# A convolution stage with a written VectorE order, norm terms with an operand in PSUM, and column sums one gate projection earlier

## The chip, the cores and the metric

The kernel runs on 1 core of one Trainium2 chip. The metric is the device time of one execution in microseconds. The core's engines work side by side and meet through semaphores: TensorE (PE in the profile, its weight loads PEld), VectorE (DVE), ScalarE (ACT), GpSimd (POOL) and SyncE (SP), which issues the transfers here.

## What is computed

Two layers over 256 tokens of width 2048: forgetting attention, then a causal convolution module. The change is in the second layer:

```python
def conv_mixer(h, w_in, b_in, dw, dw_b, ln_g, ln_b, w_out):
    proj = h @ w_in + b_in                       # h = rmsnorm(x) here; w_in is 2048 x 6144
    a, b, gate = jnp.split(proj, [C, 2 * C], axis=-1)        # C = 2048
    u = a * jax.nn.sigmoid(b)
    u = lax.conv_general_dilated(u, dw, ..., padding=[(30, 0)], feature_group_count=C) + dw_b   # 31 taps a channel
    u = jax.nn.silu(layernorm(u, ln_g, ln_b))    # mean and variance over the 2048 channels
    y = u * jax.nn.silu(gate)
    return y @ w_out
```

The result is added to the layer's input, and a final rmsnorm follows.

## The kernel before

The second layer holds channels on the partitions: a channel tile (`ct`, 16 of them) is 128 channels by 256 tokens. Each weight tile of 128 x 2048 numbers comes from memory into `raw`, ScalarE rounds it to `hi` (L93), VectorE or GpSimd makes the rest `lo` (L94), and TensorE does three matmuls for each product: hi by hi, hi by the activations' rest, lo by hi (L161). `hi` and `lo` have three buffers each. The order of TensorE is the order in which the program is written, for the whole kernel.

The stage runs in groups. Group 0 and group 1 are 128 channels wide, then come pairs 1 to 7 of 256 channels (two channel tiles). Each projects `b`, then `a`; VectorE evicts both (`eb`, `ea`, L669, times the token scales `rb1`), ScalarE makes the sigmoid of `b` in PSUM (L683), VectorE the gated input `u` (L684), into a PSUM bank with 30 zeros ahead (L682), and then 31 taps for each channel tile (L694, the first of group 0 and 1 L692). ScalarE writes the finished tile to `dall` (L699) and its square to `sq` (L705); GpSimd sums these over the tiles into `accd` and `accs`, VectorE the last ones (L712). To keep the squares small, the mean over the first 128 channels is taken with one matmul (`mean_shift`, `pm`, L722) and taken off everywhere (`negs`).

After the pairs come the four gate chunks of 512 channels (16 steps each, a step is a 128-deep slice of the weights), whose evicts `eg` go through a SiLU, and then the out projection (L188 to L190, `po`). The column sums `ln_rows` (`pstat`, L618) are put by an agenda (`at`) at step 9.5 of chunk 3; behind them come VectorE's small rows, GpSimd's power `rl` (L759), the row scales (VectorE's diagonals `dg`, TensorE's `bc_rl` and `bc_mr`, VectorE's copies to `rlb` and `mrb`) and the norm terms `t` with the results `y1a` and `y1b`.

TensorE has 4 banks of PSUM for projections and 4 for the rest. VectorE's order is a scheduler's: the evicts and the gated inputs stand under `tc.high_priority(2000)`, which puts them among the taps. GpSimd's order is the written one from chunk 3 on.

Of the kernel before, what the change touches and what calls it, by code (L numbers as in the profile page):

```python
# [19 lines left out]
MASK = 1.0e30  # L20
RMS_EPS = 1e-6
LN_EPS = 1e-5
LN_STEP = 9.5
LN_ROWS = 1.5


@with_exitstack
def tile_hybrid_trunk(
# [33 lines left out]
    def bank(name):  # L62
        return psa.tile([P, 512], F32, tag="at", name=name)
# [105 lines left out]
    def proj_t(wv, c0, width, ah, al, lo_engs, pieces=1, banks_apart=False, ahead=False, made=()):  # L169

        ps = banks_t(width)
        tail = []
        for kt, hv, lv in stream(wv, c0, width, lo_engs, pieces, ahead, made):
            if banks_apart and kt >= KT - 2048 // width:

                products_t(ps, kt, hv, lv, ah, al, range(2))
                tail.append((kt, hv, lv))
            else:
                products_t(ps, kt, hv, lv, ah, al, range(width // P))
        for kt, hv, lv in tail:  # L180
            products_t(ps, kt, hv, lv, ah, al, range(2, width // P))
        return ps
# [9 lines left out]
    def tiles(t):  # L192
        return lambda kt: t[:, kt, :]
# [468 lines left out]
    def evict(ps, width, name):  # L662

        outs = []
        for b, bank_ in enumerate(ps):
            n = min(2, width // P - 2 * b)
            e = ph.tile([P, 2, S], F32, tag="ev", name=f"{name}_{b}", bufs=4)
            with tc.high_priority(2000):
                nc.vector.tensor_tensor(  # L669
                    e[:, 0:n, :],  # L670
                    bank_[:, 0 : n * S].rearrange("p (a t) -> p a t", a=n),
                    rb1.broadcast_to([P, n, S]),
                    op=ALU.mult,
                )
# [3 lines left out]
    def conv_tile(ct, a, b, sig):

        u = bank(f"u{ct}")[:, 0 : TAPS - 1 + S]  # L680
        with tc.high_priority(2000):
            nc.vector.memset(u[:, 0 : TAPS - 1], 0.0)  # L682
            nc.scalar.activation(sig, b, AF.Sigmoid, bias=bT[:, KT + ct : KT + ct + 1])  # L683
            nc.vector.scalar_tensor_tensor(  # L684
                u[:, TAPS - 1 :], a, bT[:, ct : ct + 1], sig, op0=ALU.add, op1=ALU.mult
            )
        acc = ph.tile([P, S], F32, tag="acc", name=f"acc{ct}", bufs=3)
        for t in range(TAPS):
            w = dwT[:, t * KT + ct : t * KT + ct + 1]
            src = u[:, t : t + S]  # L690
            if t == 0 and ct < 2:
                nc.vector.tensor_scalar(acc, src, w, None, op0=ALU.mult)  # L692
            else:
                nc.vector.scalar_tensor_tensor(  # L694
                    acc, src, w, negs if t == 0 else acc, op0=ALU.mult, op1=ALU.add
                )
        bcol = dwbT[:, ct : ct + 1]
        d = dall[:, ct, :]
        nc.scalar.activation(d, acc, AF.Identity, bias=bcol)  # L699
        if ct < 2:  # L700
            shifted.append(d)
            return
        if ct % 2 == 0:
            sqs.append(ph.tile([P, 2, S], F32, tag="sq", name=f"sq{ct}", bufs=3))
        nc.scalar.activation(sqs[-1][:, ct % 2, :], acc, AF.Square, bias=bcol)  # L705
        if ct % 2 and ct < KT - 1:
            nc.gpsimd.tensor_tensor(accd, dall[:, 0:2, :] if ct == 3 else accd, dall[:, ct - 1 : ct + 1, :], op=ALU.add)
            nc.gpsimd.tensor_tensor(accs, accs, sqs[-1], op=ALU.add)
        if ct >= KT - 3:

            for acc, last in ((accd, d), (accs, sqs[-1][:, ct % 2, :])):
                nc.vector.tensor_tensor(  # L712
                    acc[:, 0, :], acc[:, 0, :], acc[:, 1, :] if ct == KT - 3 else last, op=ALU.add
                )

    shifted = []
    sqs = []

    def mean_shift():

        pm = bank("pm")[:, 0:S]
        nc.tensor.matmul(pm, ones, dall[:, 0, :], start=True, stop=True)  # L722
        nc.vector.tensor_scalar(negs, pm, -1.0 / P, None, op0=ALU.mult)
        for i, d in enumerate(shifted):
            nc.vector.tensor_tensor(d, d, negs, op=ALU.add)
            nc.scalar.activation(accs[:, i, :], d, AF.Square)

    def conv_group(c0, width):
        eng = VE if c0 < 256 else GE
        pc = 4 if c0 < 256 else 1  # L730
        pb = proj_t(w_cin, D + c0, width, tiles(ah), tiles(al), eng, pc)
        pa = None if c0 else proj_t(w_cin, c0, width, tiles(ah), tiles(al), eng, pc)
# [12 lines left out]
    rlb = ph.tile([P, 1, S], F32, name="rlb", bufs=1)  # L745
    mrb = ph.tile([P, 1, S], F32, name="mrb", bufs=1)

    def ln_rows():
        st = const.tile([P, 4], F32, name="st")
# [3 lines left out]
        nc.vector.tensor_scalar(st, pstat[:, 0:4], 1.0 / D, None, op0=ALU.mult)  # L753
        var = const.tile([P, 2], F32, name="var")
        nc.vector.tensor_tensor(var, st[:, 0:2], st[:, 0:2], op=ALU.mult)
        nc.vector.tensor_tensor(var, st[:, 2:4], var, op=ALU.subtract)
        nc.vector.tensor_scalar(var, var, 0.0, LN_EPS, op0=ALU.max, op1=ALU.add)
# [3 lines left out]
        nc.vector.tensor_tensor(mr, st[:, 0:2], rl, op=ALU.mult)
        at(LN_ROWS, lambda: row_scales(rl, rlb[:, 0, :], "rl"))
        at(LN_ROWS, lambda: row_scales(mr, mrb[:, 0, :], "mr"))
        at(LN_ROWS + 0, lambda: [gated(cp) for cp in range(4)])
# [38 lines left out]
    while agenda:
        agenda.pop(0)[1]()
# [130 lines left out]
```

## Time and profile before

| | us |
|---|---|
| median of 3 runs | 918.09 (917.91 to 918.62) |
| the profiled execution | 918.69 |
| its span, first to last instruction | 916.9 |
| TensorE busy in the span | 883.0 (96%) |
| VectorE / ScalarE / GpSimd busy | 597.8 / 414.7 / 373.1 |
| mean granted clock of TensorE | 0.983 of full speed |

The convolution stage runs from about 511 us to the end. The page's slices of the span show TensorE full up to some 780 us, then one slice of 40 at four tenths of its time, where its clock is at six tenths, and again full until the end. VectorE is at eight to nine tenths from 530 to 830 us.

### The profile page before, as it was taken

How to read it: one execution, taken by the hardware profiler on the slowest of the kernel's cores; microseconds unless marked ns; L12 is line 12 of the kernel's file. 1: busy time of each engine (PE TensorE's matmuls, PEld its weight loads, DVE VectorE, ACT ScalarE, POOL GpSimd, SP SyncE). 2: the span in 40 equal slices, each digit the busy share in tenths (PEclk: the TensorE clock that was granted, in tenths of full speed). 3: DMA queues.
4: the chain of work that ended last, by engine and by line, in shares of the span. 5: the costliest groups of instructions: out<-in, count | busy, mean ns of one | idle time of the engine just before them, and what ended most of it. 6: DMA issues, size and time to landing. Idle time of an engine off the chain costs nothing.

```text
span 916.9 us, 15886 instructions
## 1 busy us (share of the span) xinstructions
PE 883.0 (96%) x6642; PEld 849.8 (93%) x6642; DVE 597.8 (65%) x1042; ACT 414.7 (45%) x535; POOL 373.1 (41%) x234
## 2 busy tenths in 40 slices
PE   8799999999999999999999999999999999489996
PEld 8789899999999899989999999999999999477886
DVE  5464564445544564446655789988889879898541
ACT  5453554345534453346444534434433543266531
POOL 3128343103410232103100087989889888532110
PEclk9989999999999999999999999999999999689999
DMA  9899965689799756754455745555555555226532
GB/s 215 163 179 180 232 190 146 183 180 182 144 179 186 193 141 170 184 189 167 149 185 149 230 144 179 184 185 184 185 184 184 184 184 184 92 92 212 170 124 93
DMA packets 101563, 157.71 MB, mean 172 GB/s; under 512 B 4740, under 2 KB 42740, under 8 KB 101364
## 3 DMA queue, kind: packets, MB, share of 16 engines
q1 hardware_dynamic: 101156, 155.63, 63.1%
q8 instruction: 52, 0.85, 0.4%
q10 hardware_dynamic: 336, 1.07, 0.3%
q14 instruction: 19, 0.16, 0.1%
HBM read 154.59 MB, written 2.10 MB: 171 GB/s over the span
## 4 chain that ended last, share of the span: by engine, by line
PE 84%; DVE 5%; issue 3%; SPq 2%; DMA 2%; POOL 2%; ACT 1%; POOLq 0%; DVEq 0%; ACTq 0%
PE pt L161 63%; PE pv L189 3%; PE pv L188 3%; PE pv L190 3%; PE po L189 2%; PE po L190 2%; PE po L188 2%; SPq L313 2%; DMA rawk<-in_fox_w_in_dram 1%; DVE acc L694 1%; DMA raw<-in_fox_w_in_dram 1%; POOL lo L94 1%; ACT hi L93 1%; PE sc L485 1%; DVE t L777 1%
## 5 line engine op out<-in xcount | busy, mean ns | idle before, releaser
L161 PE MATMUL pt<-ah,hi 128*128 128x256 f32 x1472 | 422.0, 287 | 6.1 <-ACT hi L93 6.1
L93 ACT ACTIVATE hi<-raw 128x2048 fp32r<-128x2048 f32 (+2 forms) x188 | 271.4, 1465 | 343.5 <-PE pt L161 182.8
L161 PE MATMUL pt<-ah,lo 128*128 128x256 f32 x1472 | 419.0, 285 | 0.2 <-DVE lo L94 0.2
L161 PE MATMUL pt<-al,hi 128*128 128x256 f32 x1472 | 418.8, 284 | 0.0
L94 DVE TENSOR_TENSOR lo<-raw,hi 128x2048 fp32r<-128x2048 f32 (+1 forms) x136 | 216.1, 1611 | 201.7 <-ACT hi L93 201.7
L161 PEld LDWEIGHTS pt<-ah,hi 128*128 128x128 f32 x1472 | 285.1, 194 | 6.6 <-ACT hi L93 6.5
L161 PEld LDWEIGHTS pt<-ah,lo 128*128 128x128 f32 x1472 | 284.7, 193 | 0.6 <-DVE lo L94 0.6
L161 PEld LDWEIGHTS pt<-al,hi 128*128 128x128 f32 x1472 | 285.1, 194 | 0.0
L94 POOL TENSOR_TENSOR lo<-raw,hi 128x2048 fp32r<-128x2048 f32 (+1 forms) x52 | 223.8, 4316 | 61.0 <-ACT hi L93 60.6
L694 DVE SCALAR_TENSOR_TENSOR acc<-u,dwT,acc 128x256 f32<-128x256 f32 x480 | 196.8, 474 | 1.4
L161 PE MATMUL pt<-yh,hi 128*128 128x256 f32 x256 | 73.3, 286 | 0.0
L161 PE MATMUL pt<-yl,hi 128*128 128x256 f32 x256 | 72.5, 283 | 0.6 <-POOL yl L94 0.6
L161 PE MATMUL pt<-yh,lo 128*128 128x256 f32 x256 | 72.5, 283 | 0.0
L479 POOL CAST la<-ones 64x256 fp32r<-64x256 f32 x16 | 6.3, 394 | 143.0 <-PE sc L488 139.0
L188 PE MATMUL pv<-hi,ah 128*128 128x512 f32 x128 | 50.1, 391 | 0.0
L161 PEld LDWEIGHTS pt<-yl,hi 128*128 128x128 f32 x256 | 49.1, 192 | 0.8 <-POOL yl L94 0.8
L189 PE MATMUL pv<-hi,al 128*128 128x512 f32 x128 | 49.8, 389 | 0.0
L190 PE MATMUL pv<-lo,ah 128*128 128x512 f32 x128 | 49.8, 389 | 0.0
L161 PEld LDWEIGHTS pt<-yh,hi 128*128 128x128 f32 x256 | 49.1, 192 | 0.0
L161 PEld LDWEIGHTS pt<-yh,lo 128*128 128x128 f32 x256 | 49.1, 192 | 0.0
L200 POOL TENSOR_TENSOR r_l<-ms_l,mhalf 128x2 f32<-128x2 f32 x2 | 1.4, 714 | 99.5 <-DVE ms_l L198 99.5
L94 POOL TENSOR_TENSOR yl<-y,yh 128x256 fp32r<-128x256 f32 x15 | 19.8, 1322 | 42.1 <-ACT yh L93 42.1
(240 smaller groups left out, 1025.1 us busy)
## 6 DMA issues: line engine op xcount, KB each, us to landing
raw<-in_fox_w_in_dram SPq DMA_DIRECT2D x60, 1024.0 KB, 6.8
raw<-in_conv_w_in_dram SPq DMA_DIRECT2D x48, 1024.0 KB, 5.2
raw<-in_fox_w_out_dram SPq DMA_DIRECT2D x16, 1024.0 KB, 5.1
raw<-in_conv_w_out_dram SPq DMA_DIRECT2D x16, 1024.0 KB, 5.1
rawk<-in_fox_w_in_dram SPq DMA_DIRECT2D x4, 512.0 KB, 12.6
xn<-in_x_dram SPq DMA_DIRECT2D x3, 512.0 KB, 11.4
rawk<-in_fox_w_in_dram SPq DMA_DIRECT2D x4, 256.0 KB, 7.2
raw<-in_fox_w_in_dram SPq DMA_DIRECT2D x2, 512.0 KB, 15.4
```

The costliest lines, as they stand in the source:

```text
L93: nc.scalar.activation(dst_hi, src, AF.Copy)
L94: lo_eng.tensor_tensor(dst_lo, src, dst_hi.bitcast(F32), op=ALU.subtract)
L161: nc.tensor.matmul(ps[nt // 2][:, (nt % 2) * S : (nt % 2 + 1) * S], w[:, nt * P : (nt + 1) * P], a(kt), start=(kt == 0 and i == 0 and nt % ...
L188: nc.tensor.matmul(ps, ah(kt)[:, ms], hv, start=first, stop=False)
L189: nc.tensor.matmul(ps, al(kt)[:, ms], hv, start=False, stop=False)
L190: nc.tensor.matmul(ps, ah(kt)[:, ms], lv, start=False, stop=last)
L200: nc.gpsimd.tensor_tensor(r, ms, mhalf, op=ALU.pow)
L313: nc.sync.dma_start(bf[0:H], fox_b_f[0].rearrange("(h o) -> h o", o=1))
L479: nc.gpsimd.tensor_copy(la[0:64], ones[0:64, 0:1].broadcast_to([64, S]))
L485: nc.tensor.matmul(sc[:, 0:S], qT[q][:, j, :], kT[k][:, j, :], start=(i == 0), stop=False)
L694: nc.vector.scalar_tensor_tensor(acc, src, w, negs if t == 0 else acc, op0=ALU.mult, op1=ALU.add)
L777: nc.vector.tensor_tensor(t, dall[:, cs, :], rlb.broadcast_to([P, 2, S]), op=ALU.mult)
```

## The change

VectorE gets a written order from group 0's evicts to the end of gate chunk 0. The taps of a pair are collected in a list (`line`) and emitted with 8 entries held back (7 taps and the closing step); then come the next pair's evicts, then the 8, then the next pair's gated inputs. In front of chunk 0's evicts 30 entries are held back. `conv_alone` (channel tiles 0 and 1) uses two accumulators in turn and adds them at the end, one operand in PSUM. `mean_shift` is called at step 7 behind group 0, which is inside group 1's a-projection, and its result stays in a bank of its own (`kept`), so the others have 3 banks. `shift` reads it there. The last pair's sums go over a PSUM bank (`pd`, `ps`). The `lo` of group 1 are made by GpSimd. The column sums are at step 10 of chunk 2, the row scales four steps later; their diagonals are made by ScalarE, the results stay in PSUM, and `t` is there too.

```diff
-LN_STEP = 9.5
-LN_ROWS = 1.5
+LN_STEP = 10
+LN_ROWS = 4
...
-    psa = ctx.enter_context(tc.tile_pool(name="psa2", bufs=4, space=bass.MemoryType.PSUM, reuse_waits="tile"))
+    psa = ctx.enter_context(tc.tile_pool(name="psa2", bufs=3, space=bass.MemoryType.PSUM, reuse_waits="tile"))
+
+    def kept_bank(name):
+
+        return psa.tile([P, 512], F32, tag="kept", name=name, bufs=1)
...
+    line = []
+
+    def emit(rest=0):
+        while len(line) > rest:
+            line.pop(0)()
...
+    def shift(ct):
+
+        d = dall[:, ct, :]
+        nc.vector.scalar_tensor_tensor(d, kept["pm"], -1.0 / P, d, op0=ALU.mult, op1=ALU.add)
+        nc.scalar.activation(accs[:, ct, :], d, AF.Square)
+
+    def conv_alone(ct, bk):
+
+        accs2 = [acc_tile(f"acc{ct}_{i}") for i in range(2)]
         for t in range(TAPS):
...
+            line.append(lambda t=t: tap(accs2[t % 2], ct, bk, t, True if t < 2 else None))
+
+        def end():
+            other = bk[:, 0:S]
+            nc.scalar.activation(other, accs2[1], AF.Identity, bias=dwbT[:, ct : ct + 1])
+            nc.vector.tensor_tensor(dall[:, ct, :], accs2[0], other, op=ALU.add)
+            if ct:
+                shift(ct)
...
+    def conv_pair(ct, bks):
+
+        pair = [(ct + i, bk, acc_tile(f"acc{ct + i}")) for i, bk in enumerate(bks)]
+        for t in range(TAPS):
+            for c, bk, acc in pair:
+                line.append(lambda c=c, bk=bk, acc=acc, t=t: tap(acc, c, bk, t, None if t else negs))
...
+                bk = pair[0][1]
+                pd, ps = bk[:, 0:S], bk[:, S : 2 * S]
+                nc.scalar.activation(pd, pair[0][2], AF.Identity, bias=dwbT[:, ct : ct + 1])
+                nc.scalar.activation(ps, pair[0][2], AF.Square, bias=dwbT[:, ct : ct + 1])
+                nc.vector.tensor_tensor(pd, pd, dall[:, ct + 1, :], op=ALU.add)
+                nc.vector.tensor_tensor(ps, ps, sq[:, 1, :], op=ALU.add)
+                nc.vector.tensor_tensor(accd[:, 0, :], pd, accd[:, 0, :], op=ALU.add)
+                nc.vector.tensor_tensor(accs[:, 0, :], ps, accs[:, 0, :], op=ALU.add)
...
     def conv_group(c0, width):
...
+        if not c0:
+            vector_order.enter_context(tc.manual_schedule(engines={mybir.EngineType.DVE}))
+        emit(8)
         b = evict(pb, width, f"eb{c0}")
...
+        a = evict(pa, width, f"ea{c0}")
+        emit()
...
+                dg = sm.tile([P, P], F32, tag="dg", name=f"dg_ln{i}_{m}")
+                nc.scalar.activation(dg, ident, AF.Copy, scale=cols[:, m : m + 1])
...
+        t = bank(f"t{cp}").rearrange("p (a t) -> p a t", a=2)
+        ts = ph.tile([P, 2, S], F32, tag="sq", name=f"ts{cp}", bufs=3)
+        nc.vector.tensor_tensor(ts, dall[:, cs, :], kept["rl"].broadcast_to([P, 2, S]), op=ALU.mult)
+        nc.vector.tensor_tensor(t, ts, kept["mr"].broadcast_to([P, 2, S]), op=ALU.subtract)
...
+    vector_order = ExitStack()
     conv_group(0, 128)
+    emit(8)
+    at(7, lambda: (emit(), mean_shift()))
     conv_group(128, 128)
-    at(13, mean_shift)
     for c in range(1, 8):
+        emit(8)
         conv_group(c * 256, 256)
...
+    emit(30)
+    gate_chunk(0)
+    emit()
+    vector_order.close()
+    gate_chunk(1)
+    at(LN_STEP, ln_rows)
+    pool_order = ctx.enter_context(ExitStack())
+    pool_order.enter_context(tc.manual_schedule(engines={mybir.EngineType.Pool}))
+    gate_chunk(2)
+    gate_chunk(3)
```

VectorE before, among the taps of pair 1 (`acc2`, `acc3`), where pair 2's a-projection is evicted:

```order
L694 SCALAR_TENSOR_TENSOR acc3_5936<-u3_5932,dwT_5312,acc3_5936 128x256
L669 TENSOR_TENSOR ea512_0_6192<-pt173_0_6083,rb1_5301 128x512
L694 SCALAR_TENSOR_TENSOR acc2_5897<-u2_5893,dwT_5312,acc2_5897 128x256
L684 SCALAR_TENSOR_TENSOR u4_6194<-ea512_0_6192,par_511,pt169_0_5972 128x256
L694 SCALAR_TENSOR_TENSOR acc2_5897<-u2_5893,dwT_5312,acc2_5897 128x256
L694 SCALAR_TENSOR_TENSOR acc3_5936<-u3_5932,dwT_5312,acc3_5936 128x256
L684 SCALAR_TENSOR_TENSOR u5_6233<-ea512_0_6192,par_511,pt169_0_5972 128x256
L694 SCALAR_TENSOR_TENSOR acc2_5897<-u2_5893,dwT_5312,acc2_5897 128x256
```

The gated inputs `u4` and `u5` stand between two taps of the pair before. The same place after, at the end of pair 1's taps:

```order
L701 SCALAR_TENSOR_TENSOR acc4_6200<-u4_6192,dwT_5312,acc4_6200 128x256
L701 SCALAR_TENSOR_TENSOR acc5_6201<-u5_6196,dwT_5312,acc5_6201 128x256
L692 MEMSET u6_6493 128x30
L694 SCALAR_TENSOR_TENSOR u6_6493<-ea768_0_6477,par_511,pt177_0_6257 128x256
L692 MEMSET u7_6497 128x30
L694 SCALAR_TENSOR_TENSOR u7_6497<-ea768_0_6477,par_511,pt177_0_6257 128x256
L705 SCALAR_TENSOR_TENSOR acc6_6501<-u6_6493,dwT_5312,negs_5315 128x256
```

These rows are one pair further on (`u6`, `u7` behind the taps of `acc4`, `acc5`); between pairs 1 and 2 they read alike. A gated input now stands behind the last tap in front of it.

ScalarE before, where the sigmoids of pair 3 (written over `pt177`) stand; `hi` are the copies of weight tiles, `dall` and `sq` close a channel tile:

```order
L705 ACTIVATE sq2_5930<-acc3_5936,par_511 128x256
L93 ACTIVATE hi186_6577<-raw185_6575 128x2048
L683 ACTIVATE pt177_0_6273<-eb768_0_6382,par_511 128x256
L93 ACTIVATE hi188_6631<-raw187_6629 128x2048
L93 ACTIVATE hi190_6688<-raw189_6686 128x2048
L683 ACTIVATE pt177_0_6273<-eb768_0_6382,par_511 128x256
L93 ACTIVATE hi192_6742<-raw191_6740 128x2048
```

And after:

```order
L93 ACTIVATE hi196_6916<-raw195_6914 128x2048
L693 ACTIVATE pt177_0_6257<-eb768_0_6475,par_511 128x256
L93 ACTIVATE hi198_6971<-raw197_6969 128x2048
L752 ACTIVATE dall_5313<-acc4_6200,par_511 128x256
L753 ACTIVATE sq4_6486<-acc4_6200,par_511 128x256
L752 ACTIVATE dall_5313<-acc5_6201,par_511 128x256
L753 ACTIVATE sq4_6486<-acc5_6201,par_511 128x256
L693 ACTIVATE pt177_0_6257<-eb768_0_6475,par_511 128x256
```

The second sigmoid of pair 3 moved from ahead of `hi192` to behind `hi198` and behind the four rows that close pair 2.

GpSimd after, at the end of gate chunk 2 (`lo240` is its last weight tile):

```order
L94 TENSOR_TENSOR lo236_8296<-raw235_8293,hi236_8295 128x2048
L94 TENSOR_TENSOR lo238_8350<-raw237_8347,hi238_8349 128x2048
L813 TENSOR_TENSOR rl_8389<-vs_8387,mhalf_90 128x2
L94 TENSOR_TENSOR lo240_8420<-raw239_8417,hi240_8419 128x2048
L94 TENSOR_TENSOR lo242_8534<-raw241_8531,hi242_8533 128x2048
```

Before, `rl` stood behind the last `lo` of chunk 3:

```order
L94 TENSOR_TENSOR lo244_8473<-raw243_8470,hi244_8472 128x2048
L94 TENSOR_TENSOR lo246_8479<-raw245_8476,hi246_8478 128x2048
L94 TENSOR_TENSOR lo248_8485<-raw247_8482,hi248_8484 128x2048
L759 TENSOR_TENSOR rl_8619<-var_8615,mhalf_90 128x2
L821 MEMSET ssn_8789 128x10
```

## Rows read from the trace of the kernel before

**Rows 1.** TensorE's waits, 520 to 917 us: us in total, times, longest.
```profile
PE pstat L618 <- DVE accd L712: 7.1, 1, 7.1
PE bc_rl L237 <- DVE dg_rl L236: 3.4, 2, 1.8
...
PE bc_mr L237 <- DVE dg_mr L236: 1.5, 1, 1.5
...
PE po L189 <- DVE y1b L94: 0.9, 1, 0.9
```

**Rows 2.** Busy time of each engine in two stretches; columns in the first line.
```profile
core 0: us, PE busy (x) PEld busy (x) DVE busy (x) ACT busy (x) POOL busy (x), PEclk, DMA share, GB/s
521.00:746.00 225.00, 225.00 (x1876) 224.94 (x1875) 200.23 (x486) 95.37 (x86) 188.47 (x49) 1.00 0.55 179
...
781.00:795.00 14.00, 6.93 (x36) 6.65 (x34) 10.62 (x20) 2.67 (x4) 4.52 (x5) 0.63 0.23 75
```

**Rows 3.** Timeline of TensorE, three stalls: start, us, instruction, [idle before <-releaser].
```profile
48.11 0.58 PE L161 MATMUL pt<-ah,hi 128*128 128x256 f32 x1 [4.80 <-ACT hi L93]
...
49.42 0.41 PE L161 MATMUL pt<-al,hi 128*128 128x256 f32 x1
49.64 0.41 PE L161 MATMUL pt<-ah,lo 128*128 128x256 f32 x1
...
53.69 0.28 PE L161 MATMUL pt<-ah,hi 128*128 128x256 f32 x1
...
788.43 1.01 PE L618 MATMUL pstat<-ones,accd 128*128 128x1 f32 x4 [7.07 <-DVE accd L712]
...
820.63 0.50 PE L188 MATMUL po<-hi,y1a 128*128 128x512 f32 x1 [2.48 <-ACT y1a L93]
```

**Rows 4.** Timeline of TensorE, the out projection's start.
```profile
809.16 0.39 PE L188 MATMUL po<-hi,y1a 128*128 128x512 f32 x1
...
825.92 0.39 PE L188 MATMUL po<-hi,y1b 128*128 128x512 f32 x1
826.15 0.39 PE L189 MATMUL po<-hi,y1b 128*128 128x512 f32 x1
```

**Rows 5.** Timeline of VectorE, 517 to 577 us.
```profile
525.42 0.49 DVE L684 SCALAR_TENSOR_TENSOR u<-ea,par,pt 128x256 f32<-128x256 f32 x1 [0.33 <-ACT pt L683]
...
530.77 5.15 DVE L694 SCALAR_TENSOR_TENSOR acc<-u,dwT,acc 128x256 f32<-128x256 f32 x10
536.18 0.42 DVE L669 TENSOR_TENSOR ea<-pt,rb 128x256 f32<-128x256 f32 x1 [0.27 <-PE pt L161]
...
556.59 3.70 DVE L725 TENSOR_TENSOR dall<-dall,negs 128x256 f32<-128x256 f32 x1
...
568.24 6.34 DVE L694 SCALAR_TENSOR_TENSOR acc<-u,dwT,acc 128x256 f32<-128x256 f32 x16
574.51 0.67 DVE L669 TENSOR_TENSOR eb<-pt,rb 128x512 f32<-128x512 f32 x1
575.11 9.48 DVE L694 SCALAR_TENSOR_TENSOR acc<-u,dwT,acc 128x256 f32<-128x256 f32 x24
```

**Rows 6.** Timeline of VectorE around the column sums.
```profile
788.35 0.43 DVE L712 TENSOR_TENSOR accs<-accs,sq 128x256 f32<-128x256 f32 x1
790.34 0.16 DVE L753 TENSOR_SCALAR st<-pstat 128x4 f32<-128x4 f32 x1 [1.56 <-PE pstat L618]
```

**Rows 7.** Timeline of ScalarE, 690 to 722 us.
```profile
697.81 1.92 ACT L93 ACTIVATE hi<-raw 128x2048 fp32r<-128x2048 f32 x1 [3.84 <-PE pt L161]
...
711.54 0.51 ACT L699 ACTIVATE dall<-acc,par 128x256 f32<-128x256 f32 x1 [0.29 <-DVE acc L694]
711.96 0.49 ACT L705 ACTIVATE sq<-acc,par 128x256 f32<-128x256 f32 x1
...
716.91 0.46 ACT L683 ACTIVATE pt<-eb,par 128x256 f32<-128x256 f32 x1
```

**Rows 8.** Timeline of GpSimd, two places.
```profile
705.57 4.64 POOL L94 TENSOR_TENSOR lo<-raw,hi 128x2048 fp32r<-128x2048 f32 x1 [0.94 <-ACT hi L93]
...
791.17 0.71 POOL L759 TENSOR_TENSOR rl<-var,mhalf 128x2 f32<-128x2 f32 x1 [9.48 <-DVE var L757]
```

More of the change, by code (lines that the diff above doesn't have):

```diff
@@ L675, in evict @@
             outs += [e[:, i, :] for i in range(n)]
         return outs
[L678 to L687, printed above, removed]
-        for t in range(TAPS):
[L689 to L714, printed above, removed]
@@ new lines, in tap, with acc_tile @@
+    def tap(acc, ct, bk, t, first):
+        w = dwT[:, t * KT + ct : t * KT + ct + 1]
+        src = bk[:, t : t + S]
+        if first is None:
+            nc.vector.scalar_tensor_tensor(acc, src, w, acc, op0=ALU.mult, op1=ALU.add)
+        elif first is True:
+            nc.vector.tensor_scalar(acc, src, w, None, op0=ALU.mult)
+        else:
+            nc.vector.scalar_tensor_tensor(acc, src, w, first, op0=ALU.mult, op1=ALU.add)
+    def acc_tile(name):
+        return ph.tile([P, S], F32, tag="acc", name=name, bufs=4)
@@ L719, in mean_shift @@
     def mean_shift():
-        pm = bank("pm")[:, 0:S]
+        pm = kept_bank("pm")[:, 0:S]
         nc.tensor.matmul(pm, ones, dall[:, 0, :], start=True, stop=True)
         nc.vector.tensor_scalar(negs, pm, -1.0 / P, None, op0=ALU.mult)
-        for i, d in enumerate(shifted):
-            nc.vector.tensor_tensor(d, d, negs, op=ALU.add)
-            nc.scalar.activation(accs[:, i, :], d, AF.Square)
-    def conv_group(c0, width):
[L729 to L732, printed above, removed]
-        b = evict(pb, width, f"eb{c0}")
-        a = evict(pa or proj_t(w_cin, c0, width, tiles(ah), tiles(al), eng), width, f"ea{c0}")
-        for i in range(width // P):
-            conv_tile(c0 // P + i, a[i], b[i], pb[i // 2][:, (i % 2) * S : (i % 2 + 1) * S])
+        kept["pm"] = pm
@@ new lines, in mean_shift, with end @@
+        shift(0)
+    def conv_pair(ct, bks):
[3 more added lines that the diff above has]
+                line.append(lambda c=c, bk=bk, acc=acc, t=t: tap(acc, c, bk, t, None if t else negs))
+        def end():
+            sq = ph.tile([P, 2, S], F32, tag="sq", name=f"sq{ct}", bufs=3)
+            for i, (c, bk, acc) in enumerate(pair):
+                bcol = dwbT[:, c : c + 1]
+                nc.scalar.activation(dall[:, c, :], acc, AF.Identity, bias=bcol)
+                nc.scalar.activation(sq[:, i, :], acc, AF.Square, bias=bcol)
+            g = nc.gpsimd
+            if ct < KT - 2:
+                g.tensor_tensor(accd, dall[:, 0:2, :] if ct == 2 else accd, dall[:, ct : ct + 2, :], op=ALU.add)
+                g.tensor_tensor(accs, accs, sq, op=ALU.add)
+            if ct == KT - 4:
+                for acc in (accd, accs):
+                    g.tensor_tensor(acc[:, 0, :], acc[:, 0, :], acc[:, 1, :], op=ALU.add)
+            if ct == KT - 2:
+                bk = pair[0][1]
[6 more added lines that the diff above has]
+                nc.vector.tensor_tensor(accs[:, 0, :], ps, accs[:, 0, :], op=ALU.add)
+        line.append(end)
@@ L738, in gate_chunk @@
     def gate_chunk(c):
-        g = evict(proj_t(w_cin, 2 * D + c * 512, 512, tiles(ah), tiles(al), GE, ahead=c == 3), 512, f"eg{c}")
+        g = evict(proj_t(w_cin, 2 * D + c * 512, 512, tiles(ah), tiles(al), GE), 512, f"eg{c}")
         for i in range(4):
@@ L752, in ln_rows, with ln_rows2 @@
         column_sums(pstat, 2, accs[:, 0, :])
[L753 to L757, printed above, removed]
+        dsum, ssum, var = pstat[:, 0:2], pstat[:, 2:4], pstat[:, 8:10]
+        mean = const.tile([P, 2], F32, name="mean")
+        nc.vector.tensor_scalar(mean, dsum, 1.0 / D, None, op0=ALU.mult)
+        msq = const.tile([P, 2], F32, name="msq")
+        nc.vector.scalar_tensor_tensor(msq, dsum, 1.0 / D, mean, op0=ALU.mult, op1=ALU.mult)
+        nc.vector.scalar_tensor_tensor(var, ssum, 1.0 / D, msq, op0=ALU.mult, op1=ALU.subtract)
+        vs = const.tile([P, 2], F32, name="vs")
+        nc.vector.tensor_scalar(vs, var, 0.0, LN_EPS, op0=ALU.max, op1=ALU.add)
         rl = const.tile([P, 2], F32, name="rl")
-        nc.gpsimd.tensor_tensor(rl, var, mhalf, op=ALU.pow)
+        nc.gpsimd.tensor_tensor(rl, vs, mhalf, op=ALU.pow)
         mr = const.tile([P, 2], F32, name="mr")
[L761 to L764, printed above, removed]
+        nc.vector.scalar_tensor_tensor(mr, dsum, 1.0 / D, rl, op0=ALU.mult, op1=ALU.mult)
+        at(LN_ROWS, lambda: ln_rows2(rl, mr))
+    def ln_rows2(rl, mr):
+        bk = kept_bank("lnb")
+        for i, cols in enumerate((rl, mr)):
+            for m in range(2):
+                dg = sm.tile([P, P], F32, tag="dg", name=f"dg_ln{i}_{m}")
+                nc.scalar.activation(dg, ident, AF.Copy, scale=cols[:, m : m + 1])
+                nc.tensor.matmul(
+                    bk[:, i * S + m * P : i * S + (m + 1) * P], ones, dg, start=True, stop=True
+                )
+        kept["rl"] = bk[:, 0:S].rearrange("p (o t) -> p o t", o=1)
+        kept["mr"] = bk[:, S : 2 * S].rearrange("p (o t) -> p o t", o=1)
+        for cp in range(4):
+            gated(cp)
     HK = KT // 2
```

49 lines of the change are left out of this document (26 added, 23 removed).

## The prediction

> **What bounds the kernel now.** I read the list of TensorE's waits first, for the second half of the span. From 520 us on it holds few rows: 7.1 us for the column sums (`pstat` waits for VectorE's `accd`), 3.4 and 1.5 us for the row scales, and short waits for `y1a` and `y1b` [rows 1]. The table by stretch says the same in another way: from 521 to 746 us TensorE is busy all 225.00 us, at full clock, with 1876 matmuls, so 0.12 us each; VectorE is busy 200.23 of them [rows 2]. TensorE is the bound there and VectorE has 11% of room. From 781 to 795 us TensorE works 6.93 of 14 us at a mean granted clock of 0.63 [rows 2]. The third thing to see is what a stall costs beyond itself: behind the 4.80 us stall at 48.11 the matmuls come 0.21 us apart (49.42, 49.64) instead of 0.12 until 53.69, and the stalls of 7.07 and 2.48 us at 788.43 and 820.63 are followed by slow stretches too [rows 3]. The granted clock's two levels are 2.4 and 1.2 GHz; the slow stretch of 5.6 us loses some 5.6 x (1 - 0.12/0.21) = 2.4 us in the first case. I use 1.9 a time, twenty such matmuls, a little under it.
>
> A mark for the end: the out projection starts at 809.16 but waits again, and its 49th matmul (the first with `y1b`) starts at 825.92, where 48 at 0.228 us would have needed 10.9 us [rows 4]. With the 0.9 us wait just behind it [rows 1], the kernel before ends as if the out projection had started at 825.92 - 10.9 + 0.9 = 816.0 and never waited. All behind that point is the same in both kernels. So I look for the same point in the changed kernel: call it E, with E = 816.0 now.
>
> **The change part by part.** *Accumulators.* The channel tiles 0 and 1 were one dependent chain: 10 taps in 5.15 us, 0.515 each; alternating taps take 6.34 us for 16 and 9.48 for 24, so 0.395 [rows 5]. 62 taps save 7.4 us of VectorE, off TensorE's path.
>
> *Column mean.* `pm` moves ahead of its place, behind 12 of the 16 steps of group 1's a-projection. That projection ends at 536.1 now (its evict is at 536.18) [rows 5], so TensorE arrives 1.44 us earlier, at 534.7. It needs `dall` of tile 0: its gated input starts at 525.42 [rows 5], taps from 525.9, 31 x 0.395 = 12.2, a ScalarE row half hidden and an add (0.5): 538.7. TensorE waits 4.0 us and `pm` takes 0.3. Let A be the end of group 1: A = 536.1 + 4.3 = 540.4, and 1.9 more if the clock falls, as in every row of [rows 3].
>
> The add behind this is priced by a row that is not its own: adds with both inputs in SBUF took 3.70 us here while GpSimd worked, while the evict of the same size out of PSUM took 0.42 [rows 5]. The changed add reads PSUM once, so I take 0.42; with 3.70 the wait would be 7.3. The Trainium skill, page "SBUF — State Buffer", section "Who interferes with whom", says that a VectorE instruction with two SBUF inputs contends with a GpSimd instruction that reads SBUF and one with at most one does not. By that rule it is 0.42; the rows agree as far as they go.
>
> *VectorE's written order, the term that decides.* Before, the evicts and gated inputs had a priority and stood among the taps as soon as TensorE was through. Now a pair's 62 taps are followed, strictly, by the next pair's gated inputs, with the evicts in front of the last 7 taps. From one pair's first tap to its last are 61 x 0.395 + 2 evicts x 0.60 (574.51 to 575.11) = 25.3 us [rows 5]. Then the second gated input waits for its sigmoid, which on ScalarE stands behind four rows (`dall`, `sq` of both tiles) that need the last taps: their pitch is 0.42 (711.54, 711.96), the sigmoid is 0.46 [rows 7], and with the input's own 0.4 the gap comes to 2.7. A pair takes VectorE 28.0 us; TensorE makes one in 23.04 (192 matmuls at 0.12).
>
> ScalarE's line adds to that: the sigmoids of three pairs stand also behind `hi` copies, and such a copy starts when TensorE frees a slot three tiles back (697.81 is one that TensorE released) [rows 7]. One pair of tiles of TensorE is 5.76 us per weight tile. Counting tiles: the second gated input of pair 1 waits for the copy of a tile whose slot is free at A + 23.04 + 5.76 = A + 28.8; copy 1.92, sigmoid, input: first tap at A + 31.75. Pair 2 waits likewise for the end of pair 3's second tile, A + 57.6: 2.3 us beyond the 28.0. Pair 3 waits for the end of pair 4, A + 92.2: 6.6 beyond. From pair 4 on VectorE is late enough that the copies don't matter. First tap of pair 7: A + 31.75 + 6 x 28.0 + 2.3 + 6.6 = A + 208.65.
>
> TensorE is now held, since it has four banks and needs the evicts and gated inputs of two projections ago. Following the banks: pair 6 waits 4.3 us, pair 7 4.9, gate chunk 0 5.0 and 4.5, chunk 1 0.5 and 4.4. The last is the one that counts: chunk 1's second bank is read by the last gated input until A + 208.65 (unheld, the chunk would start at A + 184.3). From there 22.4 us end chunk 1, at A + 231.0.
>
> *Column sums in chunk 2.* They come at its 10th step, 14.4 us on: X = A + 245.4. `accd` and `accs` are ready at A + 208.65 + 25.3, four ScalarE rows and the input's copy (2.0) and four adds (2.6) on: A + 238.5, so this wait is gone. But on GpSimd the small `rl` now stands ahead of the `lo` of chunk 2's last tile, and `rl` needs the sums. From the end of `accs` to `rl`'s end were 3.1 us (788.8 to 791.9) [rows 6, 8], `lo` takes 4.64 [rows 8]: ready at X + 7.75, wanted two steps (2.9) and the sums' own matmuls (0.8) behind X. TensorE waits 4.1, and chunk 2 ends at X + 14.2, chunk 3 (23.04) at X + 37.2. Where that cover is gone in before, the whole chain of rows and row scales stood bare (7.1 + 3.4 + 1.5); here chunk 3 covers it.
>
> *Norm terms with an operand in PSUM, scales by ScalarE, two `lo` tiles on GpSimd.* At nothing: chunk 3's 23 us of matmuls lie over them, and 5 to 10 us of VectorE would have to come back to reach TensorE. The two `lo` tiles of group 1 take 4.64 each on an engine that was idle there; bound 0 to 2.
>
> *Sum.* E = 540.4 + 245.4 + 37.2 = 823.0, that is 7.0 later. Three stalls lie on the path with no slack behind them (`pm`, chunk 1, last `lo`); a slow clock behind each adds 5.7. Nothing on that stretch hides it, though a part may be lost in later waits; I take 4: 11.0. The profiled execution was 918.69 us, span 916.9 and 1.8 around it; the median of the runs is 0.6 lower. 918.7 + 11.0 = 929.7, less 0.6: 929. Its own range is 922 (no slow clock, one of the extra waits smaller) to 934 (all three, and taps 2% slower: 6 x 61 x 0.008 = 2.9).
>
> **The rivals.** *VectorE keeps up (faster).* If the sigmoids are not late, a pair costs 61 x 0.395 + 1.2 + 0.9 = 26.2 and the first tap of pair 1 comes at A + 27.3 as in before; pair 7 starts at A + 184.5, just when TensorE wants chunk 1. Then X = A + 221.8, E = 799.4 or 17 earlier: 901, up to 907 with slow clocks. For it: VectorE had 25 us of room in 225 [rows 2] and loses 7.4 of chain and the slow SBUF adds. Against: the rows behind which the sigmoid stands are in the built order. It decides at 7 to 11 us in six pairs, 1.2 to 1.8 us a pair. Chance 0.27.
>
> *About the same.* Half of these waits: 915 to 920. Chance 0.09, of which some falls either side.
>
> *The wait moves, but not to TensorE.* If the gated inputs don't hold its banks, the sums wait instead for `accd` at A + 238.5: E = A + 238.5 + 1 + 37.2 = 817, about no change; it is part of the case above. So the change would fail to gain even if only half of my mechanism were there.
>
> *Worse.* Each held bank brings its slow clock and the late tiles delay the sigmoids in turn: 934 to 940. Chance 0.05.
>
> **How the numbers follow.** Forecast 0.59 for 922 to 934, faster 0.27, same 0.09, worse 0.05. The range 905 to 935 leaves out a good part of the faster case's lower end and the worst end. A measurement here can tell 0.2%, 1.8 us. Faster 0.29, same 0.08, slower 0.63.
>
> **What would show it.** Right: new rows in TensorE's waits, for `pm` (4 us), for VectorE's `ea` evicts and `u` in pairs 6, 7 and chunks 0 and 1 (4 to 5 each), for GpSimd's `lo` in chunk 2 (4), no wait at `pstat`; pairs 28 us apart on VectorE; the out projection starting near 823 to 829. Wrong: TensorE busy without a gap from 541 to 750, or first taps of pairs 23 to 26 us apart; then the ScalarE line was shorter than I counted. If the waits are there but the out projection starts before 816, the term of column sums is wrong.

## The result and the profile after

The changed kernel takes 934.72 us (934.12 to 935.14), the kernel before 918.36 in the same comparison: ratio 1.0177, 95% interval 1.0162 to 1.0191. It is 16.4 us slower; the forecast was 929.0, slower by about 11. The measured time lies above the forecast's own range (922 to 934), at the start of the case "worse" (934 to 940, chance 0.05), and 0.3 us inside the whole range (905 to 935). Of the four runs of the kernel with the scheduler's order below, one took 1432.41 us at a mean granted clock of 0.555 and is left out of its median.

TensorE's waits from 480 us on (us in total, times, longest), which answer to [rows 1]:

```profile
PE pt L161 <- DVE ea L672: 10.1, 3, 4.2
PE pt L161 <- DVE u L694: 7.4, 2, 4.1
PE pm L736 <- DVE dall L727: 4.4, 1, 4.4
PE pt L161 <- POOL lo L94: 2.9, 1, 2.9
PE pss L618 <- DVE sqa L628: 2.9, 1, 2.9
PE lnb L825 <- ACT dg_ln L824: 0.3, 1, 0.3
```

The waits of [rows 1] are gone, `pstat` included, and others took their place: 17.5 us for evicts (`ea`) and gated inputs (`u`), which hold TensorE's banks, 4.4 for the column mean, 2.9 for the last `lo` of chunk 2, and one that the prediction did not have, 2.9 for the sum of squares `pss` at the start of the stage. The table by stretch (columns as in [rows 2]) shows part of them: TensorE was full in these 225 us, now it is busy 207.24. The 17.8 missing are the 4.4 for `pm` and 13.4 for `ea` and `u`; the last wait for `u` comes behind this stretch.

```profile
521.00:746.00 225.00, 207.24 (x1637) 206.03 (x1636) 184.20 (x472) 82.29 (x73) 168.75 (x45) 0.94 0.48 157
```

VectorE's timeline (start, us, row, [idle before <-releaser]), the first taps of the seven pairs:

```profile
579.14 0.87 DVE L705 SCALAR_TENSOR_TENSOR acc<-u,dwT,negs 128x256 f32<-128x256 f32 x2
...
609.54 0.87 DVE L705 SCALAR_TENSOR_TENSOR acc<-u,dwT,negs 128x256 f32<-128x256 f32 x2
...
644.10 0.87 DVE L705 SCALAR_TENSOR_TENSOR acc<-u,dwT,negs 128x256 f32<-128x256 f32 x2
...
671.82 0.87 DVE L705 SCALAR_TENSOR_TENSOR acc<-u,dwT,negs 128x256 f32<-128x256 f32 x2
...
699.53 0.87 DVE L705 SCALAR_TENSOR_TENSOR acc<-u,dwT,negs 128x256 f32<-128x256 f32 x2
...
727.25 0.87 DVE L705 SCALAR_TENSOR_TENSOR acc<-u,dwT,negs 128x256 f32<-128x256 f32 x2
...
756.95 0.87 DVE L705 SCALAR_TENSOR_TENSOR acc<-u,dwT,negs 128x256 f32<-128x256 f32 x2
```

The intervals are 30.40, 34.56, then three of 27.7, and 29.70 us; the prediction counted 30.3, 34.6 and 28.0 four times. TensorE's timeline at the points that the sum went by:

```profile
543.27 1.22 PE L736 MATMUL pm<-dall,ones 128*128 128x256 f32 x2 [4.36 <-DVE dall L727]
...
757.10 0.58 PE L161 MATMUL pt<-ah,hi 128*128 128x256 f32 x1 [4.09 <-DVE u L694]
...
795.18 0.50 PE L618 MATMUL pstat<-ones,accd 128*128 128x1 f32 x4
...
802.29 0.39 PE L161 MATMUL pt<-ah,lo 128*128 128x256 f32 x1 [2.94 <-POOL lo L94]
802.51 0.28 PE L161 MATMUL pt<-ah,hi 128*128 128x256 f32 x1
802.63 0.28 PE L161 MATMUL pt<-al,hi 128*128 128x256 f32 x1
...
832.42 0.39 PE L188 MATMUL po<-hi,y1a 128*128 128x512 f32 x1
```

VectorE's last row ahead of the sums, `accs`, is through at 787.4, so nothing is waited for at 795.18:

```profile
786.96 0.41 DVE L770 TENSOR_TENSOR accs<-u,accs 128x256 f32<-128x256 f32 x1
```

The out projection starts at 832.42 and never waits behind that: E moved from 816.0 to 832.4, by 16.4 us. The spans of the two profiled executions differ by 15.4 (932.3 and 916.9), so the mark of 816.0 was about 1 us early: from 832.42 to the end of its span the changed kernel needs 99.9 us, and 99.9 ahead of its own end the kernel before is at 817.0. Apart from that the point E carries the whole difference; what is left is why it is 832.4 and not 823 to 829, and whether the written order is the cause that the prediction made of it.

### The profile page after: what moved, and what is told of

Its sections match the earlier page's. It is cut to its first block, busy times and chain, and to the rows that moved or that the text cites. A ratio compares the mean times of both kernels' runs of the same rounds, so it can differ in the third digit from the quotient of the medians.

```text
span 932.3 us, 15889 instructions
## 1 busy us (share of the span) xinstructions
PE 887.5 (95%) x6642; PEld 855.5 (92%) x6642; DVE 564.7 (61%) x1031; ACT 415.6 (45%) x538; POOL 384.1 (41%) x238
## 5 line engine op out<-in xcount | busy, mean ns | idle before, releaser
L161 PE MATMUL pt<-ah,hi 128*128 128x256 f32 x1472 | 426.3, 290 | 23.2 <-DVE ea L672 10.1
L94 DVE TENSOR_TENSOR lo<-raw,hi 128x2048 fp32r<-128x2048 f32 (+1 forms) x131 | 211.7, 1639 | 204.0 <-ACT hi L93 203.9
L161 PEld LDWEIGHTS pt<-ah,hi 128*128 128x128 f32 x1472 | 288.8, 196 | 24.8 <-ACT pt L693 10.7
L161 PEld LDWEIGHTS pt<-ah,lo 128*128 128x128 f32 x1472 | 288.4, 196 | 3.8 <-POOL lo L94 3.1
L94 POOL TENSOR_TENSOR lo<-raw,hi 128x2048 fp32r<-128x2048 f32 (+1 forms) x54 | 231.4, 4292 | 142.6 <-ACT hi L93 142.6
L161 PEld LDWEIGHTS pt<-al,hi 128*128 128x128 f32 x1472 | 289.0, 196 | 0.1
L701 DVE SCALAR_TENSOR_TENSOR acc<-u,dwT,acc 128x256 f32<-128x256 f32 x478 | 188.7, 476 | 0.0
L94 POOL TENSOR_TENSOR q<-e,q 128x256 fp32r<-128x256 f32 x8 | 11.1, 1414 | 56.3 <-ACT q L93 56.3
## 6 DMA issues: line engine op xcount, KB each, us to landing
rawk<-in_fox_w_in_dram SPq DMA_DIRECT2D x4, 512.0 KB, 12.3
raw<-in_fox_w_in_dram SPq DMA_DIRECT2D x2, 512.0 KB, 15.4
```

What stands on the lines that cost most here:

```text
L94: lo_eng.tensor_tensor(dst_lo, src, dst_hi.bitcast(F32), op=ALU.subtract)
L161: nc.tensor.matmul(ps[nt // 2][:, (nt % 2) * S : (nt % 2 + 1) * S], w[:, nt * P : (nt + 1) * P], a(kt), start=(kt == 0 and i == 0 and nt % ...
L701: nc.vector.scalar_tensor_tensor(acc, src, w, acc, op0=ALU.mult, op1=ALU.add)
```

## Experiments

Times are medians; each ratio is against the kernel before, run on the same chip.

**One part alone: the `lo` tiles of group 1 on GpSimd.** The wait at `pss` was new. The kernel before, with that part of the change only:

```diff
-        eng = VE if c0 < 256 else GE
-        pc = 4 if c0 < 256 else 1
+        eng = GE if c0 else VE
+        pc = 1 if c0 else 4
```

> The kernel before with one part of the change alone: the two lo tiles of group 1 are made by GpSimd in one piece each. Theory (GpSimd's lo blocks VectorE's al rows, which read two operands from SBUF): the last two al rows take 4 to 5 us together instead of 0.87, TensorE waits some 3 us for the sum of squares and runs slowly behind it, and the time rises by 3.5 to 4.5 us, to about 922. Rival (the late start of the stage in the changed kernel has to do with VectorE's written order or the PSUM banks): al stays at 0.87 and the time at 918.4.

925.27 us, ratio 1.0067 (1.0043 to 1.0090). It shows the wait of 2.9 us at `pss`. VectorE's timeline in this kernel:

```profile
510.03 0.88 DVE L225 SCALAR_TENSOR_TENSOR al<-hT,gT,ah 128x256 fp32r<-128x256 f32 x2 [0.58 <-ACT ah L224]
513.84 4.91 DVE L225 SCALAR_TENSOR_TENSOR al<-hT,gT,ah 128x256 fp32r<-128x256 f32 x2 [1.59 <-ACT ah L224]
```

Two such rows take 0.88 us, and the next two 4.91. In the changed kernel it is 4.92, and GpSimd's timeline there has the reason:

```profile
513.34 4.59 POOL L94 TENSOR_TENSOR lo<-raw,hi 128x2048 fp32r<-128x2048 f32 x1 [74.15 <-ACT hi L93]
```

`lo` runs from 513.34 to 517.93. Of the two `al` rows, which read two operands from SBUF, the first starts at 513.69, takes 4.53 us and ends 0.3 us behind `lo`; the second takes 0.47. This is a case for the rule of the Trainium skill, page "SBUF — State Buffer", section "Who interferes with whom", which the prediction used for the adds of `dall` alone: a VectorE instruction with two SBUF inputs contends with a GpSimd instruction that reads SBUF, and the ports that the two share are an exclusive lock. The trace agrees: the row that came 0.35 us behind `lo` was not through before it, and `lo` kept its 4.59 us.

The time rose by 6.7 us and not by the 3.5 to 4.5 expected. The slow stretch behind `pss` lasts 5.5 us in this run (521.1 to 526.6, matmuls 0.21 apart), and the column sums start 5.9 us later than in the kernel before, at 794.30. The four runs spread from 922.88 to 927.21.

**The same part undone in the changed kernel.** Group 1's first `lo` by VectorE in four pieces, projected ahead of the written order (the mean keeps its place, which is step 3 now that the b-projection is already counted):

```diff
-        pb = proj_t(w_cin, D + c0, width, tiles(ah), tiles(al), eng, 1 if c0 else 4)
+        pb = early.pop() if early else proj_t(w_cin, D + c0, width, tiles(ah), tiles(al), eng, 1 if c0 else 4)
...
+            early.append(proj_t(w_cin, D + 128, 128, tiles(ah), tiles(al), VE, 4))
...
-    at(7, lambda: (emit(), mean_shift()))
+    at(3, lambda: (emit(), mean_shift()))
```

> The changed kernel with group 1's first lo tile made by VectorE in four pieces again, ahead of the written order. Theory: al is back at 0.87, no wait at the sum of squares, all behind it 4.2 us earlier: 930 to 931. Rival (VectorE's written order bounds the stage whatever its start): less than 1.5 us gained.

932.34 us, ratio 1.0144 (1.0127 to 1.0160): 2.4 us better, between the two. The first tap of pair 7 is at 752.51, 4.4 us earlier, so the start does arrive there. The rest went to the clock, in two places. Behind the wait of 4.10 us for the last gated input the matmuls stay 0.21 apart until 758.8, 5.8 us instead of 2.5 in the changed kernel, and the sums start 3.0 us earlier (792.19). The second place is behind the wait for the last `lo`, and the out projection starts 1.5 us earlier (830.94). TensorE's timeline there, in this kernel:

```profile
799.30 0.39 PE L161 MATMUL pt<-ah,lo 128*128 128x256 f32 x1 [2.95 <-POOL lo L94]
...
800.14 0.42 PE L161 MATMUL pt<-al,hi 128*128 128x256 f32 x1
800.36 0.41 PE L161 MATMUL pt<-ah,lo 128*128 128x256 f32 x1
...
804.40 0.78 PE L828 MATMUL lnb<-dg_ln,ones 128*128 128x128 f32 x4 [0.27 <-ACT dg_ln L827]
```

The stall is 2.95 us long, and from 799.8 to 803.1 the matmuls come 0.21 apart, at the lower clock. In the changed kernel the stall of 2.94 us at 802.29 has matmuls 0.12 apart behind it (802.51, 802.63). Two stalls of one length, one with a slow stretch and one without.

**The mean four steps later.** `pm` in pair 1's b-projection instead of group 1's a-projection:

```diff
-    at(7, lambda: (emit(), mean_shift()))
+    at(11, mean_shift)
     conv_group(128, 128)
```

> The changed kernel with the column mean four steps later, in pair 1's b-projection. Theory: the wait at pm (4.4) falls under 1 us and the slow stretch behind it goes; all of it reaches the end, since TensorE's and VectorE's later times hang on group 1's end: 928 to 930. Rival (only part arrives, as with the lo tile, where 4.4 us at the start became 2.4 at the end because a slow clock came back behind a later wait): 931 to 933.

927.52 us, ratio 1.0090 (1.0073 to 1.0106): 7.2 us better, a little more than expected. `pm` waits for nothing, pair 7 starts at 749.45, 7.5 us earlier, and the out projection at 824.90. The early mean cost its 4.4 us and its slow stretch, all of it to the end.

**One of the two gated inputs ahead of the last taps.** This aims at the term that decided the forecast:

```diff
-        emit()
         n = width // P
-        bks = [
-            gated_input(c0 // P + i, a[i], b[i], pb[i // 2][:, (i % 2) * S : (i % 2 + 1) * S]) for i in range(n)
-        ]
+        bks = []
+        for i in range(n):
+            emit(0 if i == n - 1 else 8)
+            bks.append(gated_input(c0 // P + i, a[i], b[i], pb[i // 2][:, (i % 2) * S : (i % 2 + 1) * S]))
```

> The changed kernel with one row pair moved: the first gated input of a pair stands ahead of the last 7 taps of the pair in front, the second stays behind them. Theory (each hand-over between pairs stands bare, since the second sigmoid waits on ScalarE for the closing rows and for the first gated input): first taps of pairs 26.7 us apart instead of 27.7 to 34.6, pair 7 some 17 us earlier, TensorE's waits for ea and u fall from 17.5 to under 6 us, time 917 to 923. Rival (the taps and evicts alone are too much for a written order, the evicts behind 55 taps hold the banks): the intervals stay above 27 us and the time above 930.

933.51 us, ratio 1.0164 (1.0143 to 1.0184). The first taps of pairs are 28.8, 34.6, 28.8, 26.8, 27.0 and 30.1 us apart: only two of six come near the theory's 26.7. TensorE still waits 16.2 us for `u`, and pair 7 starts 3.7 us earlier, not 17. VectorE's timeline, where pairs 3 and 4 begin:

```profile
636.73 0.49 DVE L694 SCALAR_TENSOR_TENSOR u<-ea,par,pt 128x256 f32<-128x256 f32 x1 [7.82 <-ACT pt L693]
...
665.53 0.49 DVE L694 SCALAR_TENSOR_TENSOR u<-ea,par,pt 128x256 f32<-128x256 f32 x1 [2.06 <-ACT pt L693]
```

And ScalarE's timeline, where pair 3 begins:

```profile
634.42 1.92 ACT L93 ACTIVATE hi<-raw 128x2048 fp32r<-128x2048 f32 x1 [3.84 <-PE pt L161]
636.24 0.46 ACT L693 ACTIVATE pt<-eb,par 128x256 f32<-128x256 f32 x1
637.25 0.48 ACT L693 ACTIVATE pt<-eb,par 128x256 f32<-128x256 f32 x1 [0.56 <-DVE u L694]
```

The wait for the sigmoid is not gone; it stands 7 taps earlier. The first sigmoid still stands behind an `hi` copy, which waits for TensorE, and the second waits for the first gated input (`u` L694). The copies come every 5.76 us, one weight tile of TensorE, and the intervals of 28.8 and 34.6 are 5 and 6 of these: there TensorE's own pace, by way of ScalarE's line, sets when the next pair begins. Moving one VectorE row doesn't shorten a hand-over whose last link is ScalarE's line.

**The scheduler's order given back, all else as changed.**

```diff
-            vector_order.enter_context(tc.manual_schedule(engines={mybir.EngineType.DVE}))
...
+            with tc.high_priority(2000):
                 nc.vector.tensor_tensor(
...
+        with tc.high_priority(2000):
+            nc.vector.memset(u[:, 0 : TAPS - 1], 0.0)
+            nc.scalar.activation(sig, b, AF.Sigmoid, bias=bT[:, KT + ct : KT + ct + 1])
```

> The changed kernel with VectorE's order left to the scheduler and the priority of evicts and gated inputs given back; all else as changed. Theory (the written order is what holds TensorE): no waits of TensorE for ea or u, which leaves the late start (4.2), the wait at pm and the one for the last lo: 905 to 913. Rival (three PSUM banks for the gated inputs hold TensorE under any order): waits for u stay, above 925.

926.75 us, ratio 1.0093 (1.0070 to 1.0115). TensorE's waits:

```profile
PE pstat L618 <- DVE accd L771: 17.1, 1, 17.1
PE pm L738 <- DVE dall L729: 5.0, 1, 5.0
PE pss L618 <- DVE sqa L628: 2.9, 1, 2.9
PE pt L161 <- POOL lo L94: 0.6, 1, 0.6
```

No wait for `ea` or `u`: the order of the changed kernel does hold the banks, and three banks for the inputs do not. The edit gives ScalarE's sigmoids their priority back too, as the kernel before had it; the two were not taken apart. The time falls by 8.0 us, not by 22 to 30, for 17.1 us of the waits came back in one piece at the sums. VectorE's sums are ready no earlier than under the written order (787.4 there): `accd` is through at 789.4, `accs` at 789.7.

```profile
788.93 0.42 DVE L771 TENSOR_TENSOR accd<-u,accd 128x256 f32<-128x256 f32 x1
```

Under this order VectorE loses its time in another way: from 565 to 790 us it idles 15.7 us for `ea`, 8.0 for `eb` and 6.1 for `eg`, evicts that stand in its line before TensorE is through. So my second theory: with the sums in chunk 2, VectorE's end is the bound, and 22 steps of TensorE (6 of chunk 2, 16 of chunk 3) come behind it. Before, 6.5 did.

**The sums alone, in the kernel before.** Step 10 of chunk 2, with GpSimd's written order from there:

```diff
-LN_STEP = 9.5
-LN_ROWS = 1.5
+LN_STEP = 10
+LN_ROWS = 4
...
-        if c == 3:
+        if c == 2:
```

> The kernel before with one part of the change alone: column sums at step 10 of gate chunk 2, row scales four steps on, GpSimd's written order from chunk 2. Theory (VectorE's convolution ends near 788 in every version, so sums in chunk 2 leave 22 steps of TensorE behind that end instead of 6.5): TensorE, not held before, arrives at 758 and waits about 31 us for accd, the out projection starts at 825 to 828, time 926 to 931. Rival (the written order alone makes the change slow): a wait that is covered, 915 to 921.

936.07 us, ratio 1.0172 (1.0140 to 1.0203): this one part, without VectorE's written order, costs as much as the whole change. TensorE's waits, the first two:

```profile
PE pstat L618 <- DVE accd L712: 20.5, 1, 20.5
PE bc_rl L237 <- DVE dg_rl L236: 5.7, 2, 4.0
```

The wait is 20.5 and not 31, since VectorE ends at 777.7 here: the move also takes chunk 2's evicts and the 4.85 us `accs` row out of its way, which I had not counted. The row scales, which read SBUF alone beside GpSimd's `lo`, eat that up: 9.1 us for the two `dg_rl`. The out projection starts at 825.4, as expected, but then needs 108.6 us to the end of the span. The kernel before needs 107.7 and the changed kernel 99.9, which the expectation left out. The edit holds the place of the sums, the later row scales and GpSimd's order from chunk 2; how much each costs, this run doesn't tell.

**The sums ten steps later, under either order.** At step 4 of chunk 3, in the changed kernel and in `sched_order`:

```diff
-LN_STEP = 10
+LN_STEP = 20
```

> The changed kernel with one part moved: the column sums ten steps later, at step 4 of gate chunk 3; the written order stays. Theory (under the written order TensorE is late itself, so the place of the sums hardly matters): no wait for accd in either place; the wait for the last lo of chunk 2 (2.9) goes, 930 to 933. Rival (the place of the sums is what costs, whatever the order): 920 to 925.

> sched_order with the column sums ten steps later, at step 4 of gate chunk 3. Theory: TensorE arrives at 787 and waits 1 to 4 us instead of 17; the out projection can start at 808 to 812, time 909 to 914. Rival (the norm chain behind the sums is then bare, as in the kernel before): the out projection waits for y1a or y1b and the gain over sched_order is under 7 us, above 920.

| us (ratio to before) | sums in chunk 2 | sums at step 4 of chunk 3 |
|---|---|---|
| written order | 934.72 (1.0177) | 932.57 (1.0141; 1.0124 to 1.0158) |
| scheduler's order | 926.75 (1.0093) | 916.31 (0.9968; 0.9955 to 0.9981) |

Undoing the order alone gives 8.0 us, moving the sums alone 2.1, both 18.4 (by the ratios, each against the kernel before on its own chip: 7.7, 3.3 and 19.2). Under the written order TensorE is late itself (795.18 at the sums where `accs` is ready at 787.4), and the place of the sums hardly matters; under the scheduler's order it is early, and they hold it. Each cause hides behind the other. The last corner is 2 us above what was expected, since TensorE still waits 6.9 us for `accd` there:

```profile
PE pstat L618 <- DVE accd L771: 6.9, 1, 6.9
```

**All that the runs point to.** The two parts at the start undone as well, first under the scheduler's order, then under the written one (with the first gated input early). The edits are those above; in both, the mean goes to `at(7, mean_shift)` ahead of group 1, since its b-projection is already counted there:

```diff
-    at(7, lambda: (emit(), mean_shift()))
+    at(7, mean_shift)
     conv_group(128, 128)
```

> sched_sums_later with group 1's first lo tile made by VectorE and the column mean four steps later (in pair 1's b-projection). Theory (each of the two costs its wait and a slow stretch at the start, which VectorE's end follows): no wait for the sum of squares, none or under 1 us at pm, VectorE's convolution ends 5 to 8 us earlier, 903 to 908. Rival (VectorE's end does not follow the start, since it waits for the evicts in between): under 3 us better than sched_sums_later.

905.80 us, ratio 0.9851 (0.9831 to 0.9870): 10.5 us better than without the two, about what they cost at the start. VectorE's end follows the start: `accd` at 780.76 instead of 790.81.

> The written order kept, with all that the other runs point to: the first gated input ahead of the last 7 taps, group 1's first lo tile on VectorE, the mean four steps later, the sums at step 4 of chunk 3. Theory (a written order in which gated inputs follow the taps holds TensorE, so the sums come at 795 or later however early VectorE is through): waits for u stay at 10 us or more, 914 to 920. Rival (the order was never the matter): as sched_best, 903 to 908.

918.10 us, ratio 0.9990 (0.9979 to 1.0000). With the sums out of the way the written order costs 12.3 us; `pstat` waits for nothing, `accs` is ready at 777.9, and TensorE reaches the sums at 794.38, held by `u` for 16.4 us.

`sched_best` still waits 6.9 us at the sums, so they went further into chunk 3, by two and by four steps (`LN_STEP` 22 and 24 in place of 20):

> sched_best with the column sums two steps later, at step 6 of chunk 3. Theory (the 6.9 us wait at the sums can be covered by steps of chunk 3 as long as the norm chain still ends before the out projection): wait 4, 903 to 905. Rival (GpSimd's power then holds back the last lo tile, or the out projection waits for y1a): no gain, 905 to 908.

> sched_best with the column sums four steps later, at step 8 of chunk 3. Theory: wait at the sums 1 to 2 us, slow stretch shorter, 900 to 903, if y1a is ready some 17 us behind the sums. Rival: the out projection waits for y1a or y1b, 904 to 908.

903.72 us, ratio 0.9828 (0.9813 to 0.9844), and 900.68 us, ratio 0.9797 (0.9782 to 0.9811). Both are as expected: two steps later take 2.9 us off the wait each time (6.9, 4.0, 1.1). The last is 18.4 us faster than the kernel before and the best of all. Its waits from 480 us on:

```profile
PE po L188 <- ACT y1a L93: 1.4, 1, 1.4
PE pstat L618 <- DVE accd L771: 1.1, 1, 1.1
PE lnb L830 <- ACT dg_ln L829: 0.9, 1, 0.9
PE pm L738 <- DVE dall L729: 0.8, 1, 0.8
PE po L189 <- DVE y1a L94: 0.2, 1, 0.2
```

Both sides of the place show in it: 1.1 us at the sums, 1.4 us where the out projection now waits for `y1a`. From 521 to 746 us TensorE is busy 224.09 of 225.00. The new accumulators, the norm terms in PSUM and ScalarE's diagonals are all in it, so none of them keeps the kernel from being faster; what each is worth by itself no run shows.

## Why the prediction came out right, and where its account was wrong

**The sum, step by step.** The end of group 1, A: 540.4 predicted, 546.7 measured. Of the 6.3 us, 4.2 are the step "two `lo` tiles on GpSimd", which was put at nothing with a bound of 0 to 2: 2.9 us of wait and a slow stretch behind it. I looked at GpSimd being idle there and not at who reads SBUF beside it; the rule that I weighed for one row applied to this one. The rest is 0.4 at `pm`, whose wait of 4.36 was predicted as 4.0, and 1.7 of the slow stretch behind it. From A to pair 7's first tap: 208.65 predicted, 210.3 measured (the last interval is 29.70, since the gated inputs wait for ScalarE's sigmoids once more, 1.66 and 1.46). From there to the sums 36.75 predicted, 38.2 measured, from the slow stretch in chunk 1. From the sums to E 37.2 predicted, 37.24 measured; as the wait for `lo` was 2.94 and not 4.1, the rest of that stretch was counted about 1.2 too short, and that the two cancel is luck.

So E came 9.4 us behind the sum's 823.0: 4.2 from the `lo` tiles, 3.2 from the slow clock behind two of the three stalls, for which 4 were allowed, and 2 from small terms. The `lo` tiles are the term that failed: with them counted, the forecast would have been near 933. That the time is inside the whole range even so is luck, for its upper end was 0.3 us away. The case "worse" had its range right, but for another reason: held banks do bring slow stretches (behind the wait that ends at 667.08 the matmuls come 0.21 us apart for some 3.6 us), yet until chunk 1 VectorE sets the pace, and its pairs stay 27.7 us apart.

**The mechanism.** VectorE's side came as counted: the six intervals are within 0.3 us of the prediction but for the last. The waits for `ea` and `u` stand where they were predicted, at pairs 6 and 7 and chunks 0 and 1, at three quarters of the size (17.5 us where 23.6 were counted); the last, which sets the time, is 4.09 for 4.4. Giving the scheduler's order back, the sigmoids' priority with it, removes them all. Whether the written VectorE order would still hold the banks if the sigmoids alone had their priority back, no run shows.

**What it was wrong about** is what would happen without these waits. The column sums were booked as a term whose wait "is gone" and whose chain chunk 3 covers. It is gone only because TensorE is late. The run of the sums alone in the kernel before (936.07) shows that this part can cost the full amount by itself, and the table of four shows that the order's share is 8.0 us as long as the sums stand in chunk 2. The rival "VectorE keeps up", given 901 to 907 and a chance of 0.27, counted on TensorE not being held; where it isn't, the time is 926.75. Its pair of 26.2 us was not reached by any order: under the scheduler's, pairs take 27 to 33, and two intervals with the first input early take 26.8 and 27.0. The rival "the wait moves, but not to TensorE", in which the sums wait for `accd` instead, was the right one, and its price (E = 817) was too low by 10: the out projection started at 827.6, for `accd` was through at 789.4 and not at 778.9, which was A + 238.5 of an A without the 4.2 and the slow clock.

**ScalarE's line.** Rows 7 were read rightly as to size: the gap between pairs is 2.6 us in the three undisturbed intervals, 2.7 predicted. That the closing rows are the cause was argued, and is only half of it: the second sigmoid also waits for the first gated input, which reads the same bank, and the first stands behind `hi` copies. The run that moved the first input shows that taking away the one leaves the other.

## What to carry to other kernels

Where two engines run side by side and meet at one point, ask what each order does to the other's arrival there: a stall that one edit removes may only be waiting behind a second one, and a table of both edits, alone and together, shows it where single runs don't. Put a meeting point where the slower engine will be through, with just enough work behind it to cover the chain that follows; here each step too early was about 1.4 us of wait for the faster engine. An idle engine is not a free one if its long instruction and another engine's short one read the same memory.

## What the runs showed of the hardware

A wait of TensorE of about 2.9 us is not priced by its length: behind one of 2.94 us the matmuls came 0.12 us apart, behind one of 2.95, in a kernel that differs only at the start of the stage, 0.21 for some 3.3 us, and behind the 2.90 at `pss` 0.21 as well, from 1.4 us on (to 524.3, in the changed kernel):

```profile
519.72 0.61 PE L618 MATMUL pss<-ones,sqa 128*128 128x1 f32 x4 [2.90 <-DVE sqa L628]
...
521.55 0.41 PE L161 MATMUL pt<-ah,hi 128*128 128x256 f32 x1
521.76 0.41 PE L161 MATMUL pt<-al,hi 128*128 128x256 f32 x1
```

And the norm rows with an operand in PSUM keep their 0.69 us while GpSimd's `lo` runs; in the changed kernel:

```profile
806.71 0.69 DVE L845 TENSOR_TENSOR ts<-dall,lnb 128x512 f32<-128x512 f32 x1 [8.81 <-PE lnb L825]
807.43 0.69 DVE L846 TENSOR_TENSOR t<-ts,lnb 128x512 f32<-128x512 f32 x1
```

GpSimd worked without a gap from 797.68 to 811.34 there:

```profile
797.68 13.66 POOL L94 TENSOR_TENSOR lo<-raw,hi 128x2048 fp32r<-128x2048 f32 x3
```
